# One ScalarE table load per run of tanh in a hybrid RWKV-7 and attention block

## The chip, the cores and the metric

The kernel runs on one core of a Trainium2 chip. A core has five engines that run on their own and meet at semaphores: TensorE (PE in the rows; its weight loads are PEld), VectorE (DVE), ScalarE (ACT), GpSimd (POOL) and SyncE (SP), which only issues DMA transfers here. ScalarE and POOL issue some DMAs too. The metric is the device time of one execution in microseconds (us), lower is better.

## The reference

One layer of a block over T = 528 tokens (512 of the input behind 16 learned ones) with 1024 features, all in float32:

```python
u = rmsnorm(h, norm_mix)
proj = u @ w_in                      # 5384 columns: RWKV, attention, two gates
y_rw = rwkv7_branch(...)             # 8 heads of 64: delta rule over time, group norm
y_fx = fox_branch(...)               # 8 heads of 64: softmax(q k' / 8 + F_q - F_k) v
merged = sigmoid(gA) * (y_rw @ w_out_rw) + sigmoid(gB) * (y_fx @ w_out_fx)
h = h + merged @ w_o
z = rmsnorm(h, norm_mlp)
h = h + square(relu(z @ w_up)) @ w_down
```

The functions that matter here are those that ScalarE evaluates from a table. The RWKV branch has `tanh` and `sigmoid` (decay, in-context rate and gate) and normalises its keys by a root. The attention branch normalises every head of q and k by a root and takes `exp` in the softmax. F is the running sum of `log_sigmoid`.

## The kernel before

**Tables.** The kernel writes a sigmoid as `0.5 tanh(x/2) + 0.5` and a reciprocal root as `exp(-0.5 ln(x))`. ScalarE holds one set of functions at a time. `natural_log_exp_and_others` has both logarithm and exponential; tanh stands in another set, which also has the exponential. Where the function of the next instruction isn't in the set that is held, the compiler puts an `ACT_TABLE_LOAD` ahead of it. The kernel also places loads itself: `pinned(prev)` (L253 to L257) issues a load of `natural_log_exp_and_others`, ordered behind the instruction `prev`, and its callers order their first logarithm behind that load. The callers are `normed` (L527, the root for q and k of one pair of attention heads, Ln at L528 and Exp at L530), `Pair.keys` (L710, Ln at L711 and Exp at L712) and the end of the mixing stage (L1080).

**Stages.** From 0 to 40 us the kernel normalises the input. From 40 to about 480 us one long stage computes 24 projections of features, 16 of gates, the RWKV branch and the attention. From there to about 577 us come the two output projections and the second norm, and after that the MLP, which is TensorE's work almost without a break.

**The long stage** is made of streams (Python generators) that a planner takes turns with: `projections` (matmuls at L476; their weights are split into a high and a low part, `whi` by ScalarE's cast at L447 and `wlo` by GpSimd at L448), `recurrent` for four pairs of RWKV heads, `chain` (the recurrence over nine chunks of 64 tokens, L871 to L920), `group_norm` (L928 to L954), `fox_features` (q and k) and `attention`. The planner fixes the order of TensorE's instructions by hand. On the other engines the framework's scheduler orders the instructions by priority and its own estimate of time, so a load more or less can change that order.

**Names.** In `Pair.keys`: `okk` the keys, `sq` their squares and then the root, `tm` the shifted copy that L306 makes of a projection in PSUM (`pj`), which VectorE's L307 combines (`orr` for r, `ov` for v); L715, L719 to L721 and L730 to L732 build the recurrence's factors. In `chain`, per chunk: matmul L887 into `pch`, VectorE copies `Rs` (L889), matmul L893, VectorE copies `uv` (L895), matmul L908, VectorE adds `SP` (L910), ScalarE prepares the next `uv` (L875) and `SP` (L903) and takes out `y_rw` (L920). In `group_norm`: sums L930, mean L931, subtraction L932, ScalarE's squares `ysq` (L934), sums L936, a root by iteration (L937, L220 to L227), scaling L939. In attention: L591 and L589 work on scores `psc`, L594 is the softmax's Exp, L614 and L626 are small copies from PSUM. L1022 are DMAs that ScalarE issues for sums of the last stage's weights, and L487 takes out a gate's projection (`gt`).

Of the kernel before, what the change touches and what calls it, by code (L numbers as in the profile page):

```python
# [13 lines left out]
AF = mybir.ActivationFunctionType  # L14
# [174 lines left out]
def kernel(ctx, tc, ht, x, win, par, cst, gain, lora, wout, wo, wup, wdn, out, dbg=None):  # L189
    nc = tc.nc  # L190
    dbg = dbg or {}
    mm = nc.tensor.matmul
    act = nc.scalar.activation
# [17 lines left out]
    prh = cp.tile([128, 4, 4], F32, name="prh")  # L211
# [28 lines left out]
    def load_w(src, low=(V, V)):  # L240

        return [load_h(src[:, 512 * j:512 * j + 512], low[j], "w", (4, 4, 4)) for j in range(2)]

    def wk(w, k):

        return [x[:, 128 * (k % 4):128 * (k % 4) + 128] for x in w[k // 4]]

    def after(ins, prev):

        tc.add_manual_dep(ins.ins, prev.ins.name, mybir.DependencyInfo(mybir.DependencyClass.NoSync, mybir.DependencyReason.DATA),  # L250
                          reason="one accumulation at a time")

    def pinned(prev):  # L253

        p = nc.scalar.preload_act_table_set("natural_log_exp_and_others")
        after(p, prev)
        return p  # L257

    def split(hi, lo, x):
        A.copy(hi, x)  # L260
# [2 lines left out]
    def passes(w, x):  # L263
        return ((w[0], x[0]), (w[0], x[1]), (w[1], x[0]))
# [6 lines left out]
    with ExitStack() as st:  # L271
# [6 lines left out]
        def psm(name="psm"):  # L278
            return ps.tile([128, 512], F32, name=name, tag="sm", bufs=4)
# [135 lines left out]
        def banks(n):  # L415
            return ck.ring("sm", n, 4)
# [80 lines left out]
        def fox_features():  # L497
            for p in range(4):
# [19 lines left out]
                def normed(d, parts, gcol):  # L518
                    yield d["in"]
                    f, sq = d["f"], d["sq"]  # L520
                    yield lambda: max(ck.ready(sq), banks(len(parts)))
                    pin = None
                    for a0, a1 in parts:
                        pq = psm("pssq")[:, :a1 - a0]
                        for hs in hss:
                            mm(pq[hs], ones_blk[hs, hs], sq[hs, a0:a1], start=True, stop=True)
                        pin = pin or pinned(d["s"])  # L527
                        after(act(sq[:, a0:a1], pq, AF.Ln, bias=eps, scale=1.0 / 64), pin)  # L528
                    c0 = parts[0][0]
                    act(sq[:, c0:], sq[:, c0:], AF.Exp, scale=-0.5)  # L530
                    V.scalar_tensor_tensor(f, f, gcol, sq[:, c0:], ALU.mult, ALU.mult)
                    return f
# [107 lines left out]
        def pad(t):  # L640
            G.memset(t[:, :PADT], 0.0)
            return t[:, PADT:]

        def load_lora(p, part, bufs):
            raw = rp.tile([128, 128], F32, name="lraw", tag="yT")
            nc.sync.dma_start(raw, lora[p][:, 128 * part:128 * part + 128])
            lw = [wp.tile([128, 128], F32R, name=f"lw{part}{i}", bufs=bufs) for i in range(2)]
            split(lw[0], lw[1], raw)
            return lw
# [3 lines left out]
        class Pair:  # L653
# [20 lines left out]
            def decay(self):  # L674
                p = self.p
                lw = load_lora(p, 0, 1)

                self.sg = sg = rp.tile([128, TP], F32, name="sg")
                self.tha = rp.tile([128, TP], F32, name="tha")
                dst = [pad(sg), pad(self.tha)]  # L680
                for a0, a1 in ((0, HT), (HT, T)):
                    yield lambda: max(ck.ready(*lw), banks(2))
                    pos = [psm("pup")[:, :HT] for i in range(2)]
                    for n, (wi, xi) in enumerate(((0, 0), (0, 1), (1, 0))):
                        for po, hs in zip(pos, hss):
                            mm(po, lw[wi][hs], (lhi, llo)[xi][hs, 0, a0:a1], start=n == 0, stop=n == 2)
                    for i in range(2):
                        act(dst[i][:, a0:a1], pos[i], AF.Tanh, bias=prh[:, i, p:p + 1], scale=0.5)
                V.tensor_scalar(dst[0], dst[0], 0.5, 0.5, ALU.mult, ALU.add)
                self.lc = lc = rp.tile([128, TP], F32, name="lc")  # L690
                V.tensor_tensor_scan(lc, smask.rearrange("p a b -> p (a b)"), sg, 0.0, ALU.mult, ALU.add)
                self.P = P = rp.tile([128, NCH, 64], F32, name="P")
                act(P.rearrange("p a b -> p (a b)"), lc, AF.Exp, scale=-CDEC)
                act(lc, lc, AF.Exp, scale=CDEC)
                self.pend = rp.tile([128, NCH], F32, name="pend", bufs=4)
                V.tensor_copy(self.pend, P[:, :, 63])

            def keys(self):

                p = self.p  # L700
                okr, thr, kp, pinv = self.okk[:, PADT:], self.tha[:, PADT:], self.sg, v9(self.lc)
                self.sq = sq = rp.tile([128, TP], F32, name="sq")
                s_ = act(sq[:, :T], okr, AF.Square, scale=self.col(C_KK))
                yield lambda: max(ck.ready(sq), banks(2))
                for hc in (slice(0, HT), slice(HT, T)):
                    pq = psm("pkk")[:, :HT]
                    for hs in hss:
                        mm(pq[hs], ones_blk[hs, hs], sq[hs, hc], start=True, stop=True)
                    V.tensor_scalar(sq[:, hc], pq, 1e-24, None, ALU.max)
                pin = pinned(s_)  # L710
                after(act(sq[:, :T], sq[:, :T], AF.Ln), pin)  # L711
                act(sq[:, :T], sq[:, :T], AF.Exp, scale=-0.5)  # L712
                V.tensor_scalar(kp[:, PADT:], thr, prh[:, 2, p:p + 1], prh[:, 3, p:p + 1], ALU.mult, ALU.add)
                V.tensor_tensor(kp[:, PADT:], kp[:, PADT:], okr, ALU.mult)
                V.scalar_tensor_tensor(okr, okr, self.col(C_KK), sq[:, :T], ALU.mult, ALU.mult)  # L715
                kkn, kp3, tha3 = v9(self.okk), v9(kp), v9(self.tha)

                self.BK = BK = rp.tile([128, NCH, 3, 64], F32, name="BK", tag="BK")
                V.scalar_tensor_tensor(BK[:, :, 2, :], kkn, 0.5, pinv, ALU.mult, ALU.mult)  # L719
                V.scalar_tensor_tensor(BK[:, :, 0, :], tha3, 1.0, BK[:, :, 2, :], ALU.add, ALU.mult)  # L720
                A.copy(BK[:, :, 2, :], BK[:, :, 0, :])  # L721
                G.tensor_tensor(BK[:, :, 1, :], kp3, pinv, ALU.mult)
# [317 lines left out]
    def ppo():  # L1040
        return ps.tile([128, 512], F32, name="po")
# [4 lines left out]
    with ExitStack() as st:  # L1046
# [3 lines left out]
                split(yhi[:, 4 * j + k, :], ylo[:, 4 * j + k, :], src[:, k, :])  # L1050
        mhi = mp.tile([128, KB, S], F32R, name="mhi")
        mlo = mp.tile([128, KB, S], F32R, name="mlo")
        for m in range(KB):
            w = load_w(wout[m])
            pp = []
            for br in range(2):
                g = mp.tile([128, S], F32, name=f"gl{br}", bufs=2)
                nc.sync.dma_start(g, gates_d[8 * br + m])
                act(g, g, AF.Tanh, scale=0.5)
                po = ppo()  # L1060
                n = 0
                for k in range(4 * br, 4 * br + 4):
                    for a, b in passes(wk(w, k), (yhi, ylo)):
                        mm(po, a, b[:, k, :], start=n == 0, stop=n == 11)  # L1064
                        n += 1
                V.scalar_tensor_tensor(g, g, 1.0, po, ALU.add, ALU.mult)
                pp.append(g)
            G.tensor_tensor(pp[0], pp[0], pp[1], ALU.add)
            merged = act(mhi[:, m, :], pp[0], AF.Copy, scale=0.5)
            V.scalar_tensor_tensor(mlo[:, m, :], pp[0], 0.5, mhi[:, m, :].bitcast(F32), ALU.mult, ALU.subtract)  # L1070
# [7 lines left out]
        zhi = hp.tile([128, KB, S], F32R, name="zhi", tag="zhi")  # L1078
        zlo = hp.tile([128, KB, S], F32R, name="zlo", tag="zlo")
        pin = pinned(merged)  # L1080
        early = []
        for j in range(2):
# [53 lines left out]
    with ExitStack() as st:  # L1136
# [50 lines left out]
        for p0, n_pairs in zip(FIRST, SLICES):  # L1187
# [4 lines left out]
            if p0 == 0:  # L1192

                ws, pos = early + [load_w(wup[2])], [ppo() for i in range(3)]
# [169 lines left out]
```

## Time and profile before

| | |
|---|---|
| median of 3 runs | 913.06 us |
| lowest and highest of them | 909.12 and 915.47 us |
| profiled execution, device time | 908.14 us |
| its span in the profile | 906.1 us |
| mean granted TensorE clock | 0.976 |
| TensorE busy | 862.7 us (95%) |
| VectorE busy | 594.3 us (66%) |
| ScalarE busy | 462.1 us (51%) |

The profile is one execution. A row of the timeline gives start, duration, engine, source line, operation, what is written from what, and in square brackets how long the engine had been idle and on whom it waited. The chain of waits follows the work that ended last back from the end; time on it is time of the kernel, time beside it is not. In the view by stretches the columns behind each stretch are its length, the busy time of PE, PEld, DVE, ACT and POOL with counts, the granted TensorE clock, the share of the DMA engines and GB/s.

### The profile page before, as it was taken

What the parts mean: (1) busy time and instruction counts of PE and PEld (TensorE: products, weight loads), DVE (VectorE), ACT (ScalarE), POOL (GpSimd) and SP (SyncE); (2) the same over time, 40 slices, a digit from 0 to 9 for tenths busy, and PEclk for the clock granted to TensorE, in tenths of its full rate; (3) what the DMA queues carried; (4) which work ended last, traced back from release to release, by engine and by line L of the source; (5) the groups of instructions that cost most, each with busy time, mean ns of one, the idle gap of its engine ahead of it and who ended that gap; (6) DMA issues with size and microseconds to landing.
All of it is one profiled execution on the core that took longest, in us unless ns stands there. A gap on an engine that the chain in (4) does not pass through costs nothing.

```text
span 906.1 us, 15737 instructions
## 1 busy us (share of the span) xinstructions
PE 862.7 (95%) x5896; PEld 702.6 (78%) x5896; DVE 594.3 (66%) x1168; ACT 462.1 (51%) x937; POOL 177.2 (20%) x169
## 2 busy tenths in 40 slices
PE   7889898999899999998989999999999999999998
PEld 6878786767797777676857877988888888888886
DVE  7965894447968794455476756377556675566776
ACT  7837243786355532675364644255444554344542
POOL 1154552223544353322301210000000000000000
PEclk9999998999999999999988999999999999999999
DMA  6223547475753467674685643034632366522564
GB/s 211 69 73 96 139 103 207 108 168 136 164 141 97 113 188 182 164 188 106 164 249 186 206 160 95 1 93 147 194 113 93 96 194 192 151 99 94 152 214 169
DMA packets 69771, 129.46 MB, mean 143 GB/s; under 512 B 6840, under 2 KB 7992, under 8 KB 69696
## 3 DMA queue, kind: packets, MB, share of 16 engines
q1 hardware_dynamic: 52288, 94.91, 32.9%
q0 software_dynamic: 8704, 16.78, 11.6%
q10 hardware_dynamic: 8704, 16.78, 5.6%
q8 instruction: 46, 0.75, 0.3%
q14 instruction: 29, 0.24, 0.1%
HBM read 122.13 MB, written 39.86 MB: 179 GB/s over the span
## 4 chain that ended last, share of the span: by engine, by line
PE 72%; DVE 15%; ACT 3%; issue 3%; DMA 2%; POOLq 0%; POOL 0%; ACTq 0%; SPq 0%; DVEq 0%
PE po L1143 19%; PE pj L476 16%; PE po L1233 12%; PE pd L1233 5%; PE po L1064 3%; PE po L1113 2%; PE pw L828 2%; DVE tmp L810 1%; PE psc L580 1%; PE py L625 1%; DVE AX L822 1%; PE pbt L776 1%; DVE Tt L822 1%; DVE AX L811 1%; DVE L L730 1%
## 5 line engine op out<-in xcount | busy, mean ns | idle before, releaser
L237 DVE TENSOR_TENSOR wlo<-wraw,whi 128x512 fp32r<-128x512 f32 x200 | 140.3, 708 | 95.8 <-ACT whi L236 95.5
L236 ACT CAST whi<-wraw 128x512 fp32r<-128x512 f32 x200 | 123.7, 621 | 135.8 <-PE po L1143 43.0
L476 PE MATMUL pj<-uhi,whi 128*128 128x264 f32 (+1 forms) x480 | 170.0, 354 | 11.0 <-DVE orr L307 3.9
L476 PE MATMUL pj<-ulo,whi 128*128 128x264 f32 (+1 forms) x480 | 157.5, 328 | 0.6 <-DVE ulo L390 0.6
L476 PE MATMUL pj<-uhi,wlo 128*128 128x264 f32 (+1 forms) x480 | 156.9, 327 | 0.0
L448 POOL TENSOR_TENSOR wlo<-wraw,whi 128x512 fp32r<-128x512 f32 x76 | 104.4, 1383 | 162.2 <-ACT whi L447 143.6
L476 PEld LDWEIGHTS pj<-uhi,whi 128*128 128x128 f32 x480 | 93.1, 194 | 32.7 <-issue 11.3
L476 PEld LDWEIGHTS pj<-uhi,wlo 128*128 128x128 f32 x480 | 93.4, 195 | 7.3
L476 PEld LDWEIGHTS pj<-ulo,whi 128*128 128x128 f32 x480 | 93.6, 195 | 5.4 <-DVE ulo L390 1.1
L1143 PE MATMUL po<-zhi,whi 128*128 128x512 f32 (+1 forms) x248 | 94.8, 382 | 0.0
L1143 PE MATMUL po<-zlo,whi 128*128 128x512 f32 (+1 forms) x248 | 94.8, 382 | 0.0
L1143 PE MATMUL po<-zhi,wlo 128*128 128x512 f32 (+1 forms) x248 | 94.8, 382 | 0.0
L447 ACT CAST whi<-wraw 128x512 fp32r<-128x512 f32 x80 | 49.2, 618 | 45.0 <-PE pj L476 27.3
L1233 PE MATMUL po<-wlo,fhi 128*128 128x512 f32 x160 | 62.4, 390 | 0.0
L1233 PE MATMUL po<-whi,flo 128*128 128x512 f32 x160 | 62.3, 389 | 0.0
L1233 PE MATMUL po<-whi,fhi 128*128 128x512 f32 x160 | 62.2, 389 | 0.0
L1143 PEld LDWEIGHTS po<-zhi,wlo 128*128 128x128 f32 x248 | 46.6, 188 | 9.1
L1143 PEld LDWEIGHTS po<-zlo,whi 128*128 128x128 f32 x248 | 46.6, 188 | 9.0
L1143 PEld LDWEIGHTS po<-zhi,whi 128*128 128x128 f32 x248 | 46.6, 188 | 8.9
L1155 ACT CAST fhi<-R 128x768 fp32r<-128x768 f32 (+1 forms) x32 | 30.2, 943 | 24.0 <-DVE R L1162 13.6
L1156 DVE TENSOR_TENSOR flo<-R,fhi 128x768 fp32r<-128x768 f32 (+1 forms) x32 | 34.8, 1089 | 7.8 <-ACT fhi L1155 7.8
L1233 PEld LDWEIGHTS po<-wlo,fhi 128*128 128x128 f32 x160 | 30.0, 188 | 6.5 <-DVE wlo L237 0.3
(292 smaller groups left out, 1658.9 us busy)
## 6 DMA issues: line engine op xcount, KB each, us to landing
wraw<-in_win SPq DMA_DIRECT2D x84, 256.0 KB, 3.0
tsum<-in_wdn ACTq DMA_DIRECT2D x32, 512.0 KB, 4.3
wraw<-in_wup SPq DMA_DIRECT2D x64, 256.0 KB, 2.6
wraw<-tsum SPq DMA_DIRECT2D x64, 256.0 KB, 2.8
wraw<-in_wdn SPq DMA_DIRECT2D x48, 256.0 KB, 2.7
tsum<-in_wdn POOLq DMA_DIRECT2D x16, 512.0 KB, 7.6
tsum<-tsum POOLq DMA_DIRECT2D x16, 512.0 KB, 6.3
gd<-gt SPq DMA_DIRECT2D x16, 256.0 KB, 2.3
```

The lines of the kernel that those rows point to most:

```text
L236: A.copy(hi, raw)
L237: low.tensor_tensor(lo, raw, hi.bitcast(F32), ALU.subtract)
L447: A.copy(hi, raw)
L448: low.tensor_tensor(lo, raw, hi.bitcast(F32), ALU.subtract)
L476: mm(po, a, b[:, k, a0:a1], start=n == 0, stop=n == 23)
L822: V.tensor_copy(dst[rs_, :, o:o + 32], src[rs_, :, :n2].rearrange("p t n -> p n t"))
L828: mm(ps_[hs, n - b0, :], lhs(n)[hs], rhs(n)[hs], start=True, stop=True)
L1064: mm(po, a, b[:, k, :], start=n == 0, stop=n == 11)
L1143: mm(po[:, t0:t1], a, b[:, k, t0:t1], start=n == 0, stop=n == 23)
L1155: A.copy(fhi[:, j, a:b], R[:, a:b])
L1156: V.tensor_tensor(flo[:, j, a:b], R[:, a:b], fhi[:, j, a:b].bitcast(F32), ALU.subtract)
L1233: mm(x[i], a[:, k, left, 128 * i:128 * i + 128], c, start=start and k == 0 and n == 0, stop=stop and k == n_pairs - 1 and n == 2)
```

## The change

A list keeps the tanh instructions that were issued since the kernel's last load. `pinned` issues a load only if that list isn't empty or if there has been none yet; otherwise it hands back the load that was issued last, and the callers order their logarithm behind that one. A new load is ordered behind all the tanh in the list. The tanh of the recurrent stream (L688) goes through the new helper. Ahead of the output projections, whose tanh (L1059) doesn't go through it, the remembered load is forgotten, so that L1080 issues one.

```diff
+    table = {"tanh": [], "pin": None}
+
+    def tanh(*args, **kw):
+        x = act(*args, func=AF.Tanh, **kw)
+        table["tanh"].append(x)
+        return x
+
     def pinned(prev):
 
-        p = nc.scalar.preload_act_table_set("natural_log_exp_and_others")
-        after(p, prev)
-        return p
+        if table["tanh"] or table["pin"] is None:
+            p = nc.scalar.preload_act_table_set("natural_log_exp_and_others")
+            after(p, prev)
+            for x in table["tanh"]:
+                after(p, x)
+            table["tanh"], table["pin"] = [], p
+        return table["pin"]
...
-                        act(dst[i][:, a0:a1], pos[i], AF.Tanh, bias=prh[:, i, p:p + 1], scale=0.5)
+                        tanh(dst[i][:, a0:a1], pos[i], bias=prh[:, i, p:p + 1], scale=0.5)
...
         mlo = mp.tile([128, KB, S], F32R, name="mlo")
+        table["pin"] = None
         for m in range(KB):
```

In the built kernels ScalarE's list has 21 table loads before and 11 in the change. TensorE's, GpSimd's and SyncE's lists read alike but for line numbers; VectorE's differs in the place of a few instructions. Lines of the changed kernel stand 11 further on (12 from L1064), its own loads are L263, and the tanh of L688 and the loads ahead of them are L256. Three places, each of before and then of the change:

Place A, ScalarE, the keys of the second pair (some 85 to 97 us in the trace of before):

```order
L703 ACTIVATE sq<-okk,pr 128x528
L255 ACT_TABLE_LOAD
L1022 DMA tsum_105<-in_wdn 256x512
L711 ACTIVATE sq<-sq 128x528
L306 ACTIVATE tm<-pj,pr 128x264
L712 ACTIVATE sq<-sq 128x528
```

```order
L714 ACTIVATE sq<-okk,pr 128x528
L1033 DMA tsum_105<-in_wdn 256x512
L317 ACTIVATE tm<-pj,pr 128x264
L722 ACTIVATE sq<-sq 128x528
L723 ACTIVATE sq<-sq 128x528
```

The load is gone, and the copy `tm`, which stood between the logarithm and the exponential, stands ahead of both.

Place B, ScalarE, roots of q and k in the second attention pair, with the recurrence beside it (some 179 to 193 us):

```order
L903 ACTIVATE SP<-uv,pend 64x64 x4
L530 ACT_TABLE_LOAD
L530 ACTIVATE fsq<-fsq 128x512
L512 ACTIVATE fsq<-pj 128x264
L513 COPY ka<-pj 128x264
L447 CAST whi<-wraw 128x512
L594 ACTIVATE pe,rsum<-pe,nm 128x528
L1022 DMA tsum_107<-in_wdn 256x512
L875 COPY uv<-pvt 64x2x128 x2
L594 ACTIVATE pe,rsum<-pe,nm 128x528
L626 COPY y_fx<-py 128x128
L255 ACT_TABLE_LOAD
```

```order
L914 ACTIVATE SP<-uv,pend 64x64 x4
L541 ACTIVATE fsq<-fsq 128x512
L523 ACTIVATE fsq<-pj 128x264
L524 COPY ka<-pj 128x264
L458 CAST whi<-wraw 128x512
L1033 DMA tsum_107<-in_wdn 256x512
L886 COPY uv<-pvt 64x2x128 x2
L605 ACTIVATE pe,rsum<-pe,nm 128x528 x2
L637 COPY y_fx<-py 128x128
L458 CAST whi<-wraw 128x512
```

Ahead of the first row the compiler's load for L528 is replaced by one of the kernel's; the compiler's load for L530 and the kernel's at the end are gone. Where the latter stood, ahead of the next `SP`, there is now the cast of a weight that came seven rows later before.

VectorE at the same place:

```order
L589 TENSOR_TENSOR psc<-psc,cs 128x128
L591 ISA pe,nm<-psc,nF_1516,nm 128x256
L591 ISA nm 128x1
L531 SCALAR_TENSOR_TENSOR qa<-qa,qg_67,fsq 128x512
L889 COPY Rs<-pch 128x128
```

```order
L600 TENSOR_TENSOR psc<-psc,cs 128x128
L542 SCALAR_TENSOR_TENSOR qa<-qa,qg_67,fsq 128x512
L602 ISA pe,nm<-psc,nF_1514,nm 128x256
L602 ISA nm 128x1
L900 COPY Rs<-pch 128x128
```

The scaling of q, which needs the root, stands ahead of a reduction of scores that stood ahead of it; `Rs` comes behind both as before.

Place C, ScalarE, the root of q in the last attention pair, with a group norm beside it (some 403 to 411 us):

```order
L255 ACT_TABLE_LOAD
L528 ACTIVATE fsq<-pssq,eps 128x512
L903 ACTIVATE SP<-uv,pend 64x64 x4
L920 COPY y_rw<-pyy 128x2x64
L530 ACTIVATE fsq<-fsq 128x512
L512 ACTIVATE fsq<-pj 128x264
L513 COPY ka<-pj 128x264
L875 COPY uv<-pvt 64x2x128 x2
L626 COPY y_fx<-py 128x128
L934 ACTIVATE ysq<-y_rw 128x512
L1022 DMA tsum_119<-in_wdn 256x512
```

```order
L539 ACTIVATE fsq<-pssq,eps 128x512
L541 ACTIVATE fsq<-fsq 128x512
L914 ACTIVATE SP<-uv,pend 64x64 x4
L931 COPY y_rw<-pyy 128x2x64
L523 ACTIVATE fsq<-pj 128x264
L524 COPY ka<-pj 128x264
L886 COPY uv<-pvt 64x2x128 x2
L945 ACTIVATE ysq<-y_rw 128x512
L637 COPY y_fx<-py 128x128
L1033 DMA tsum_119<-in_wdn 256x512
```

The load is gone, the two halves of the root follow each other, and the group norm's squares `ysq` stand ahead of the copy `y_fx` instead of behind it.

VectorE at the same place:

```order
L930 TENSOR_REDUCE st_4917<-y_rw 128x8
L889 COPY Rs<-pch 128x128
L531 SCALAR_TENSOR_TENSOR qa<-qa,qg_67,fsq 128x512
L895 COPY uv<-pch 64x128 x2
L931 TENSOR_SCALAR st_4917<-st_4917 128x8
L932 TENSOR_TENSOR y_rw<-y_rw,st_4917 128x2x256
L936 TENSOR_REDUCE st_4923<-ysq 128x8
L910 TENSOR_TENSOR uv<-pch,SP 64x128 x2
```

```order
L542 SCALAR_TENSOR_TENSOR qa<-qa,qg_67,fsq 128x512
L941 TENSOR_REDUCE st_4910<-y_rw 128x8
L900 COPY Rs<-pch 128x128
L942 TENSOR_SCALAR st_4910<-st_4910 128x8
L943 TENSOR_TENSOR y_rw<-y_rw,st_4910 128x2x256
L906 COPY uv<-pch 64x128 x2
L947 TENSOR_REDUCE st_4916<-ysq 128x8
L948 TENSOR_SCALAR st_4916<-st_4916 128x8
```

The scaling of q and the copies of `uv` no longer stand between the group norm's sums and its subtraction, and `uv`'s sum (L910, L921 in the change) falls three short instructions back.

## The prediction

> **What bounds the kernel now.** I read the page's head and its chain of waits first, then ScalarE's groups by line, then the timeline around each load.
>
> ```profile
> span 906.1 us, 15737 instructions
> ...
> PE 72%; DVE 15%; ACT 3%; issue 3%; DMA 2%; POOLq 0%; POOL 0%; ACTq 0%; SPq 0%; DVEq 0%
> ```
>
> TensorE holds 72% of the chain that sets the end, VectorE 15%, ScalarE 3%. So a load costs time only where TensorE or VectorE stands and waits for what is queued behind it. The profiled execution took 908.14 us, 2.0 more than its span; the median of the runs is 913.06, 4.9 above it. I work out a difference from the profiled execution and take it off the median.
>
> ScalarE's table loads, by the line of the instruction that needs them (L255 are the kernel's own):
>
> ```profile
> L255 ACT ACT_TABLE_LOAD x13 | 16.7, 1283 | 0.2
> ...
> L688 ACT ACT_TABLE_LOAD x3 | 3.8, 1283 | 11.8 <-PE pup L686 11.8
> ...
> L379 ACT ACT_TABLE_LOAD x1 | 1.3, 1283 | 0.0
> L528 ACT ACT_TABLE_LOAD x1 | 1.3, 1283 | 0.0
> L530 ACT ACT_TABLE_LOAD x1 | 1.3, 1283 | 0.0
> L1059 ACT ACT_TABLE_LOAD x1 | 1.3, 1283 | 1.7 <-DMA gl<-gd 1.7
> ```
>
> With the first load of the program these are 21, each 1.283 us. The change leaves 11: ten go, 10 x 1.283 = 12.8 us of ScalarE's time, and that is the most that the loads by themselves can give. All ten lie in the long stage. In the chain of waits only one of them shows:
>
> ```profile
> 179.65 1.28 ACT L528
> ...
> 182.71 1.28 ACT L530
> ```
>
> The first of these two is replaced by a load of the kernel's at the same place and costs what it cost. The second goes. The other nine stand beside the chain. Seven of them I cost at nothing: behind them ScalarE waits for another engine anyway, as here behind the load for the third pair's q,
>
> ```profile
> 302.40 0.69 ACT L528 ACTIVATE fsq<-pssq,eps 128x512 f32<-128x512 f32 x1 [3.34 <-PE pssq L526]
> ```
>
> where it then stood idle for 3.34 us, more than twice a load, or what it hands on isn't what TensorE's fixed order waits for next. If that cover were gone each would cost up to 1.28 us. The two that are left matter only because the scheduler filled ScalarE's order anew around them; these are places A and C.
>
> **Place A: one copy out of the way, 0.37 us.** ScalarE, then VectorE:
>
> ```profile
> 88.68 0.65 ACT L711 ACTIVATE sq<-sq 128x528 f32<-128x528 f32 x1 [0.95 <-DVE sq L709]
> 89.23 0.47 ACT L306 ACTIVATE tm<-pj,pr 128x264 f32<-128x264 f32 x1
> 89.59 0.64 ACT L712 ACTIVATE sq<-sq 128x528 f32<-128x528 f32 x1
> ```
>
> ```profile
> 90.26 0.77 DVE L715 SCALAR_TENSOR_TENSOR okk<-okk,pr,sq 128x528 f32<-128x528 f32 x1
> ```
>
> The load ahead of L711 is covered: ScalarE then waited 0.95 us for VectorE. But L306 stood between L711 and L712 and took 89.59 - 89.23 = 0.36 of the queue. In the change it runs in that 0.95 (its matmuls stand ahead of those that L709 needs on TensorE, so its input is there). L712 ends at 90.23 and VectorE starts L715 at 90.26, so L715 and the recurrence's factors behind it come 0.37 earlier. TensorE waits for them. Bounds: 0, if a cast's `wlo` on GpSimd, which also comes earlier, holds VectorE; 0.9, if it gets out of VectorE's way. I take 0.37.
>
> **Place B: a load of 1.28 gives 0.69 us.** VectorE's order, then TensorE:
>
> ```profile
> 183.14 0.48 DVE L591 CUSTOM_DVE_ANT_0 pe<-psc,nF,nm 128x256 f32<-128x256 f32 x1
> ...
> 184.67 0.75 DVE L531 SCALAR_TENSOR_TENSOR qa<-qa,qg,fsq 128x512 f32<-128x512 f32 x1 [1.04 <-ACT fsq L530]
> 185.34 0.28 DVE L889 COPY Rs<-pch 128x128 f32<-128x128 f32 x1
> ```
>
> ```profile
> 185.68 0.45 PE L893 MATMUL pch<-Rs,Tt 64*64 64x64 f32 x8 [1.04 <-DVE Rs L889]
> ```
>
> Without the load L530 ends 1.28 earlier, and L531 can start at 184.67 - 1.28 = 183.39. In the change L591 stands behind it and no longer fills the wait: 183.39 + 0.75 + 0.48 + some 0.03 between them gives 184.65 for `Rs`, against 185.34. So TensorE's L893 comes 0.69 earlier. More than the 1.04 that TensorE waited can't come of it, and nothing comes of it if the softmax's Exp, which falls behind `uv` on ScalarE, is then late. Ends: 0 and 1.04; I take 0.69, which the rows give.
>
> The Trainium skill ("ScalarE: Activation LUTs", What ACT_TABLE_LOAD costs) gives a switch of sets 1283 ns and about 1380 ns of drain, 2.66 us in all. The row at 182.71 agrees with the first figure and shows no drain: L530 runs right behind the load in the chain. By the page the ten loads would be worth 26.6 us of ScalarE and this place its whole 1.04, an estimate.
>
> **Place C: a wait of VectorE and GpSimd, 2.28 us, and a slow clock, 1.40 us.** ScalarE first, then VectorE, GpSimd and TensorE:
>
> ```profile
> 408.61 0.74 ACT L875 COPY uv<-pvt 64x256 f32<-64x256 f32 x2
> ...
> 410.17 0.64 ACT L934 ACTIVATE ysq<-y_rw 128x512 f32<-128x512 f32 x1
> ```
>
> ```profile
> 410.84 0.69 DVE L936 TENSOR_REDUCE st<-ysq 128x8 f32<-128x512 f32 x1 [1.02 <-ACT ysq L934]
> ...
> 414.41 1.30 DVE L227 TENSOR_SCALAR rsgy<-rsgy 128x8 f32<-128x8 f32 x1
> 415.74 1.71 DVE L939 TENSOR_TENSOR y_rw<-y_rw,rsgy 128x512 f32<-128x512 f32 x1
> 417.48 0.29 DVE L889 COPY Rs<-pch 128x128 f32<-128x128 f32 x1
> ```
>
> ```profile
> 414.39 2.51 POOL L448 TENSOR_TENSOR wlo<-wraw,whi 128x512 fp32r<-128x512 f32 x2 [10.86 <-ACT whi L447]
> ```
>
> ```profile
> 417.82 0.45 PE L893 MATMUL pch<-Rs,Tt 64*64 64x64 f32 x8 [2.28 <-DVE Rs L889]
> ```
>
> With the load gone the root of q is done sooner, and the squares stand right behind L875: they start at 408.61 + 0.74 = 409.35 instead of 410.17, 0.82 earlier. (Their input, the subtraction on VectorE, now has L531 and the copies of `uv` out of its way.) The group norm's root then runs 0.82 earlier, and L227 comes at 413.59. Before, it began 0.02 behind GpSimd's two `wlo` and took 1.30 us for 8 elements a row, and L939 took 1.71 for 512, where L936 takes 0.69 for as many: both stood until GpSimd was through. At 413.59 L227 is ahead of GpSimd. That start, 414.39, hangs on ScalarE's cast, which follows the copies of `SP`, which follow L910; and L910 falls three short instructions back, at (3.57 - 0.69) / 12 = 0.24 each (410.84 to 414.41, twelve instructions behind L936), so GpSimd gains only 0.1 or so. `Rs` is then ready before TensorE needs it, and the wait of 2.28 goes whole. If GpSimd still catches them, 0.82 is left. I take 2.28.
>
> After that wait TensorE ran slow; after a shorter one in the same loop it did not. The rows are the stretch behind this wait, then the other wait with the stretch behind it:
>
> ```profile
> 418.00:422.00 4.00, 4.00 (x43) 2.58 (x42) 1.15 (x4) 2.22 (x7) 0.00 (x0) 0.65 0.96 193
> ```
>
> ```profile
> 218.47 0.45 PE L893 MATMUL pch<-Rs,Tt 64*64 64x64 f32 x8 [1.43 <-DVE Rs L889]
> ```
>
> ```profile
> 220.00:224.00 4.00, 4.00 (x52) 2.93 (x51) 2.18 (x6) 3.34 (x10) 0.53 (x1) 1.00 0.00 0
> ```
>
> The granted clock was 0.65 behind the wait of 2.28 us and 1.00 behind that of 1.43. Four microseconds at 0.65 lose 4 x 0.35 = 1.40 us. Even if only 0.82 goes, the wait is 1.46, next to the one without a loss, so I count the 1.40; the ends are 0 and 1.40.
>
> The Trainium skill ("TensorE: Matmul & The Clock Gate", Part 1: The HAM clock gate) has the clock halved after an idle window of about 3.4 us, free-running. The row shows it reduced behind 2.28 us already. By that rule taken literally a shorter wait changes nothing in the clock, and the sum would lack 1.40 us; that case is weighed among the rivals.
>
> **The sum.** 0.37 + 0.69 + 2.28 + 1.40 = 4.74 us. Behind each place the chain runs on through TensorE, whose order is unchanged, so a shift there is kept; the last 330 us are TensorE's alone. 908.14 - 4.74 = 903.4 for a run like the profiled one, 913.06 - 4.74 = 908.3 for the median.
>
> **The rivals.**
>
> - *Only the bare shifts.* GpSimd still stands in VectorE's way at C, so that 0.82 of the wait goes, and the clock falls all the same because what counts is the phase of its window. Then 0.37 + 0.69 + 0.82 = 1.88, 911.2 us. For it: GpSimd and VectorE are some 0.7 apart at the crossing, and a small delay turns it. Against: 1.46 stands next to the 1.43 that cost nothing. Chance 0.27 with all between it and the forecast's lower part.
> - *ScalarE is closer to the bound than the chain shows.* Five of the nine covered loads have work of other streams right behind them with little or no idle time. If each of these brings its 1.28, that is 5 x 1.283 = 6.4 on top, 11.2 in all, 901.9 us. All ten on the path and the terms at C would give some 896. For it: in the stretch around B ScalarE was back to back. Against: TensorE has its own work there, and the chain passes none of them. Chance 0.15.
> - *A cast blocks ScalarE, and the kernel is slower.* At B the weight's cast moves into the place of a load:
>
> ```profile
> 188.66 1.28 ACT L255 ACT_TABLE_LOAD   x1
> ...
> 194.10 0.61 ACT L447 CAST whi<-wraw 128x512 fp32r<-128x512 f32 x1
> ```
>
>   ScalarE works in order. If the buffer that this cast writes were still being read by TensorE, or its weight not yet loaded, everything behind it (`SP` and `uv` of the recurrence, the root of k) would wait, at worst until 194.10: 194.10 - 188.66 = 5.44 us, and TensorE with it. It decides against the kernel above the 4.74 that the rest gives: 913.8 us, and 916.6 if C gives only 0.82 without the clock. Against it: that the cast stood at 194.10 was the scheduler's place for it, not a wait (its row has no idle time), and with four buffers the one it writes held a weight that TensorE was half through by then. Chance 0.06.
> - *The change doesn't do what it says.* The compiler could put loads back where a logarithm meets the wrong set, as it did at L528 and L530. The order of the change shows 11 loads and none of the compiler's in front of a logarithm, so I give this no chance of its own.
>
> **How the numbers follow.** The forecast has 0.45, the bare shifts 0.27, more loads on the path 0.15, the blocked cast 0.06; 0.07 stays for the clock falling in other places once the phases have moved. The likeliest is 908.3 us. Its own range goes from the bounds of its terms, 4.74 with A at 0.9 and B at 1.04, 5.6 (907.5), to 1.88 (911.2). The runs before lay between 909.12 and 915.47, some 0.4% to either side, and that is added in part. The low end takes in most of the second rival, 901.5; the high end takes in the third's smaller price, 914.5. One per cent, 9.1 us, is about what a measurement of this kernel can tell from no change. Faster by more than that needs the second rival or the forecast with a run to run spread in its favour: 0.19. Slower by more than that, over 922.2 us, needs the blocked cast with something on top: 0.03. Within: 0.78.
>
> **What would show it.** ScalarE with 11 loads and some 449 us busy (462.1 less 12.8). At A, L306 ahead of L711, and L715 some 0.03 behind the end of L712. At B, TensorE's L893 with a wait of some 0.35 us instead of 1.04. At C, L227 in some 0.2 us, L939 near 0.7, the wait at L893 gone or under 0.5, and a clock of 1.00 in the four microseconds behind it. A span of some 901.4. The forecast is wrong if GpSimd's `wlo` still lies over L227 at C, if the clock is below 0.9 in stretches where it was 1.00, or if ScalarE stands at the moved cast with a wait for TensorE or a DMA.

## The result, and the profile after

The changed kernel takes 904.01 us (median of 11 runs, 902.41 to 907.24), the kernel before 910.57 us (11 runs): a ratio of 0.993, 95% interval 0.9907 to 0.9953. On another chip it was 906.41 against 911.6, 0.9946 (0.9918 to 0.9973). So it is half a per cent to 0.7% faster, within the one per cent for which the forecast had its largest chance. The profiled span went from 906.1 to 901.0 us, 5.1 less; the forecast was a span of 901.4 and a median of 908.3.

The page of the changed kernel, its head and its chain of waits, and then ScalarE's table loads by line (busy, mean ns | idle before):

```profile
span 901.0 us, 15730 instructions
...
PE 858.4 (95%) x5896; PEld 699.2 (78%) x5896; DVE 593.8 (66%) x1168; ACT 449.3 (50%) x927; POOL 175.9 (20%) x169
...
PE 69%; DVE 15%; DMA 4%; ACT 4%; issue 3%; POOLq 0%; POOL 0%; ACTq 0%; SPq 0%; DVEq 0%
...
L263 ACT ACT_TABLE_LOAD x5 | 6.4, 1283 | 0.1
L256 ACT ACT_TABLE_LOAD x3 | 3.8, 1283 | 12.5 <-PE pup L697 12.5
```

With three more of one each these are 11 loads, and ScalarE is 449.3 us busy: both as forecast. ScalarE lost 12.8 us of work and the kernel 5.1.

Place B and then place C in the changed kernel, by the timeline; B is TensorE alone, C is VectorE, GpSimd and TensorE:

```profile
184.73 0.40 PE L487 MATMUL pj<-uhi,wlo 128*128 128x512 f32 x1
185.26 0.45 PE L904 MATMUL pch<-Rs,Tt 64*64 64x64 f32 x8
```

```profile
412.68 0.17 DVE L227 TENSOR_SCALAR rsgy<-rsgy 128x8 f32<-128x8 f32 x1
412.89 0.69 DVE L950 TENSOR_TENSOR y_rw<-y_rw,rsgy 128x512 f32<-128x512 f32 x1
413.77 0.29 DVE L900 COPY Rs<-pch 128x128 f32<-128x128 f32 x1 [0.19 <-PE pch L898]
```

```profile
413.29 2.67 POOL L459 TENSOR_TENSOR wlo<-wraw,whi 128x512 fp32r<-128x512 f32 x2 [10.68 <-PE pj L487]
```

```profile
414.55 0.45 PE L904 MATMUL pch<-Rs,Tt 64*64 64x64 f32 x8
```

Neither row of L904 shows a wait for `Rs` any more (1.04 and 2.28 us before). L227 takes 0.17 us and the multiplication L950 0.69, where they took 1.30 and 1.71: both now start ahead of GpSimd (412.68 and 412.89 against 413.29), and it takes its turn behind them. The clock behind it is whole, in the number behind the busy times (1.00, the granted clock):

```profile
412.00:416.00 4.00, 4.00 (x41) 2.85 (x39) 2.28 (x9) 2.95 (x9) 2.71 (x3) 1.00 0.10 40
416.00:420.00 4.00, 4.00 (x52) 2.60 (x49) 1.67 (x5) 2.94 (x9) 0.76 (x1) 1.00 0.80 162
```

Place A went the other way. VectorE, GpSimd and TensorE of the changed kernel:

```profile
96.28 3.75 DVE L743 TENSOR_TENSOR L<-orr,P 64x576 f32<-64x576 f32 x2
```

```profile
98.14 1.27 POOL L459 TENSOR_TENSOR wlo<-wraw,whi 128x512 fp32r<-128x512 f32 x1 [0.37 <-ACT whi L458]
```

```profile
100.17 1.57 PE L772 MATMUL psr<-L,BK 64*128 64x128 f32 x22 [0.83 <-DVE tm L314]
```

and VectorE and GpSimd before:

```profile
96.57 2.63 DVE L732 TENSOR_TENSOR L<-orr,P 64x576 f32<-64x576 f32 x2
```

```profile
98.44 3.19 POOL L448 TENSOR_TENSOR wlo<-wraw,whi 128x512 fp32r<-128x512 f32 x2 [0.38 <-ACT whi L447]
```

VectorE's two products for `L` took 2.63 us and take 3.75. GpSimd's `wlo` got in ahead of the second one, which then stood until GpSimd was through; TensorE waits 0.83 us for what follows. Here a gain of 0.37 was forecast.

**How the places were measured.** TensorE's list is the same in all kernels here, so its nth matmul in one trace is the nth in the other. The difference of their starts moves in steps, each with a place. The table gives these steps in us against the profiled execution of the kernel before, worked out from the matmul records (A: 91 to 103 us, B: 180 to 194, C: 409 to 425), the number of clock windows at half speed (below), and the span. The rows are the kernels of the next section; a second and third row of a kernel is another profiled execution.

| kernel | A | B | C | slow windows | span |
|---|---|---|---|---|---|
| before | 0 | 0 | 0 | 12 | 906.1 |
| before, 2nd | +1.12 | -0.01 | +0.02 | 11 | 909.9 |
| changed | +0.77 | -0.77 | -3.81 | 9 | 901.0 |
| changed, 2nd | +0.76 | -0.79 | -3.80 | 12 | 907.3 |
| changed, 3rd | -0.36 | -0.78 | -3.80 | 12 | 904.1 |
| r_a | +0.01 | -0.79 | -3.80 | 7 | 898.6 |
| r_c | +0.77 | -0.79 | +1.28 | 14 | 908.0 |
| r_all | +1.11 | -0.81 | -1.47 | 8 | 906.1 |
| e_edges | +1.46 | +0.01 | -2.93 | 12 | 905.0 |
| r_rest | +0.76 | -0.79 | -3.81 | 12 | 905.4 |
| e_fixa | -0.34 | -0.78 | -3.81 | 9 | 902.2 |
| e_fixa, 2nd | -0.34 | -0.78 | -3.80 | 12 | 905.2 |
| e_mlp | +0.76 | -0.76 | -3.80 | 12 | 908.3 |

Between the places the difference is flat to some hundredths of a microsecond, but for other slow windows and smaller crossings like that of A. Spans of one kernel lie up to 6.3 us apart, so a single span tells little here, and the steps tell much. The ratios below are the recorded ones, with their 95% intervals; they aren't the quotients of the two medians given beside them, from which they differ by up to 0.4% (e_fixa: 0.9878 recorded, 0.9917 by medians).

### The profile page after: what moved, and what is told of

Read it like the earlier page. It is cut to its first block, busy times and chain, and to the rows that moved or that the text cites. A ratio compares the mean times of both kernels' runs of the same rounds, so it can differ in the third digit from the quotient of the medians.

```text
span 901.0 us, 15730 instructions
## 1 busy us (share of the span) xinstructions
PE 858.4 (95%) x5896; PEld 699.2 (78%) x5896; DVE 593.8 (66%) x1168; ACT 449.3 (50%) x927; POOL 175.9 (20%) x169
## 4 chain that ended last, share of the span: by engine, by line
PE 69%; DVE 15%; DMA 4%; ACT 4%; issue 3%; POOLq 0%; POOL 0%; ACTq 0%; SPq 0%; DVEq 0%
PE po L1155 19%; PE pj L487 16%; PE po L1245 11%; PE pd L1245 5%; PE po L1125 2%; PE po L1076 2%; PE pw L839 2%; DMA wraw<-in_wo 1%; DVE tmp L821 1%; PE py L636 1%; DVE AX L833 1%; PE pbt L787 1%; PE psc L591 1%; DVE Tt L833 1%; DVE L L743 1%
```

## The experiments

### Loads put back one place at a time

Four kernels are the changed one with a list of places at which a load is issued all the same:

```diff
-    def pinned(prev):
+    def pinned(prev, place=None):
-        if table["tanh"] or table["pin"] is None:
+        if place in KEEP or table["tanh"] or table["pin"] is None:
...
+KEEP = ("keys1",)                    # r_a
+KEEP = ("q3", "k3")                  # r_c
+KEEP = ("keys1", "k0", "q1", "k1", "keys2", "q2", "k2", "q3", "k3")   # r_all
+KEEP = ("k0", "keys2", "q2", "k2")   # r_rest
```

**r_a, the load at place A.**

> The changed kernel with one of the ten loads put back, the one ahead of the logarithm of the second pair's keys (place A). ScalarE's order there is then that of before: the copy tm between logarithm and exponential, so L715 of before comes 0.3 later again, the cast whi too, and GpSimd's wlo should start behind VectorE's second copy of the convolution's output instead of ahead of it. Theory (the crossing at A costs the change some 0.9): the load put back makes the kernel faster than the changed one, a span of about 900.1 us against 901.0, VectorE's two copies in 2.63 instead of 3.75, and TensorE's matmul that waits for gt at about 142.7 instead of 143.6. Rival (a load costs its time on ScalarE): span 901.0 + 1.28 = 902.3. No effect beyond the noise of a profile would be 901.0 within 0.3.

Ratio to before 0.9929 (0.9895 to 0.9964), median 907.17 against 912.4. At A the two products took 2.64 us and TensorE's step was +0.01, so it looks as the theory said. But the span of 898.6, below the 900.1 expected, goes with only 7 slow windows, and the next kernels showed that the load is not what decided at A.

**r_c, the two loads of the last attention pair.**

> The changed kernel with the loads ahead of q's and k's logarithm in the last attention pair put back (place C, two loads). The squares ysq then stand behind the copy y_fx again. Theory (order at C sets the crossing with GpSimd): TensorE's wait for Rs of about 2.3 us near 413 to 418 returns, and a granted clock of 0.6 to 0.8 in the 4 us behind it; L227 takes over 1 us again; the span is 901.0 + 3.8 = 904.8 us. Rival (the gain at C is the loads' own time): 2 x 1.28 = 2.6, span 903.6, with no return of the slow clock. If neither order nor load matters there, 901.0.

Ratio 0.9989 (0.9957 to 1.0022), median 910.73: with these two loads back the gain is gone to within the interval. VectorE and TensorE of r_c at C:

```profile
412.87 1.29 DVE L228 TENSOR_SCALAR rsgy<-rsgy 128x8 f32<-128x8 f32 x1
414.19 1.71 DVE L951 TENSOR_TENSOR y_rw<-y_rw,rsgy 128x512 f32<-128x512 f32 x1
```

```profile
416.28 0.69 PE L905 MATMUL pch<-Rs,Tt 64*64 64x64 f32 x8 [2.27 <-DVE Rs L901]
```

The wait is back, 2.27 us, with the old durations of both instructions, and two slow windows behind it. TensorE's step at C is 1.28 + 3.81 = 5.1 us worse than in the changed kernel; without the second slow window it would be the 3.8 of the theory. The loads' own time, 2.6, is out.

**r_all, all nine places of the kernel's own loads.** One of the nine, the second pair's q, has its load in the changed kernel too, so the trace has 19 loads, eight more than the changed kernel and two fewer than before.

> The changed kernel with all nine of its own covered loads put back; against before only place B differs, where one load of the kernel's and two of the compiler's are now one, and VectorE scales q (L531 of before) ahead of the reduction of scores (L591). It isolates B. Theory: B gives the 1.28 us of a load, because the wait of 1.04 at TensorE goes and the stages behind it are kept; at A the order of before (no loss), at C the order of before (wait 2.28 and slow clock there): span 906.1 - 1.28 = 904.8 us. The prediction's own term for B would give 906.1 - 0.69 = 905.4. Rival (each load costs its time on the path): 901.0 + 9 x 1.28 = 912.5.

Ratio 0.9973 (0.9936 to 1.001), median 909.52, span 906.1. At B the wait is gone and the step is -0.81, close to the prediction's term and not the 1.28 of a load. The rival's 912.5 (911.2 with eight loads) is out. What the order on VectorE would give at B without taking a load away was not tried. Two things were not expected. At A the products took 3.75 us although ScalarE's order there was that of before. And at C the wait was as long as before, but the clock was whole behind it (see the clock, below).

**r_rest, four of the loads costed at nothing.**

> The changed kernel with four of the loads put back that the prediction costed at nothing: before the roots of k of the first pair, of q and k of the third, and before the logarithm of the third pair's keys. Theory (behind them ScalarE waits for another engine anyway): 0 us by the loads themselves, TensorE's steps as in the changed kernel within 0.3 us up to place C, apart from slow clock; span 901.0 give or take the 1.7 us that one slow window of the clock costs. Rival (a load costs its time on ScalarE): 4 x 1.28 = 5.1 us more, 906.1.

Ratio 0.9928 (0.9902 to 0.9954), median 905.64 against 911.12 on its chip. ScalarE's loads are

```profile
L264 ACT ACT_TABLE_LOAD x9 | 11.5, 1283 | 0.1
```

9 where the changed kernel has 5, and the ratio is that of the changed kernel. Its steps at A, B and C are the changed kernel's within 0.02. The span, 905.4, lies near the rival's 906.1 and outside what the theory allowed, but it has 12 slow windows, and the changed kernel's own two profiles with 12 of them took 904.1 and 907.3. So the span decides nothing here. The steps and the ratio do: the four loads cost nothing that can be seen.

### Order alone, with all 21 loads

e_edges is the kernel before with two edges of order at C:

```diff
-                    A.copy(y_fx[:, p, 128 * i:128 * i + 128], py)
+                    taken = A.copy(y_fx[:, p, 128 * i:128 * i + 128], py)
+                    if (p, i) == (2, 3):
+                        after(taken, marked["ysq"])
...
-                    V.tensor_copy(uv[hs, 0, e], ch[hs, 1])
+                    u_ = V.tensor_copy(uv[hs, 0, e], ch[hs, 1])
+                    if (g, c, e) == (1, 5, 0):
+                        after(u_, marked["centred"])
```

> The kernel before with all its 21 loads; two edges of order are added at place C only: the copy y_fx stands behind the squares ysq, and the copy uv on VectorE behind the subtraction that makes ysq's input. Theory (C's gain is a matter of order, not of a load): GpSimd's wlo no longer catches L227, the wait of 2.28 at TensorE goes, the clock stays 1.00 behind it, and the span is 906.1 - 3.7 = 902.4 us. Rival (the load's 1.28 in front of q's root is what delays ysq, and stays): ysq comes at most 0.4 earlier, GpSimd still stands in the way, span 905.7 to 906.1.

VectorE, GpSimd and TensorE of e_edges at C:

```profile
414.99 0.17 DVE L227 TENSOR_SCALAR rsgy<-rsgy 128x8 f32<-128x8 f32 x1
415.20 1.81 DVE L949 TENSOR_TENSOR y_rw<-y_rw,rsgy 128x512 f32<-128x512 f32 x1
```

```profile
415.18 2.96 POOL L450 TENSOR_TENSOR wlo<-wraw,whi 128x512 fp32r<-128x512 f32 x2 [10.62 <-PE pj L478]
```

```profile
417.39 0.45 PE L897 MATMUL pch<-Rs,Tt 64*64 64x64 f32 x8 [0.81 <-DVE Rs L893]
```

The 8-element L227 got ahead of GpSimd, the multiplication behind it did not, by 0.02 us. The wait fell from 2.28 to 0.81 and the clock stayed whole: 2.93 of the 3.81 us came without a load removed.

ScalarE's squares and VectorE's sum for `uv`, in e_edges and then that sum in the changed kernel:

```profile
410.32 0.63 ACT L942 ACTIVATE ysq<-y_rw 128x512 f32<-128x512 f32 x1
```

```profile
412.35 0.59 DVE L916 TENSOR_TENSOR uv<-pch,SP 64x128 f32<-64x128 f32 x2 [0.47 <-PE pch L914]
```

```profile
410.45 0.59 DVE L921 TENSOR_TENSOR uv<-pch,SP 64x128 f32<-64x128 f32 x2
```

At C e_edges ran 1.03 us behind before. Put back by that, its squares began at 410.32 - 1.03 = 409.29, 0.88 earlier than before and no later than in the changed kernel (409.38, worked out below). So the load in front of q's root doesn't hold them up, and the rival, 0.4 at most, is out. What e_edges lacks of the changed kernel's gain lies behind the squares, on VectorE: there the sum for `uv` still stands ahead of the root's steps and waits 0.47 us for TensorE, and L227 comes 0.36 later than in the changed kernel, which has that sum two short instructions further back and no wait. No run moves this sum alone, so that last part is read from the rows and not shown.

The median is 908.54 against 912.4, a quotient of 0.9958, but the recorded ratio, 0.9988 (0.996 to 1.0016), doesn't separate e_edges from before. The span, 905.0 against the 902.4 expected, has as many slow windows as before, 12, but one of them lies at A. So by the steps the mechanism at C is order, as the theory had it.

### The crossing at A

> The kernel before, unchanged, for a second look at the clock. Theory (the clock is granted for windows of 3.41 us whose phase differs from one execution to the next; a window in which TensorE is busy for less than about half is followed by one at half clock): the same waits as in the first look within 0.1 us where no slow window falls, among them 2.2 to 2.3 us at place C; the slow windows lie elsewhere than in the first look, and behind the wait at C the clock is 1.00 if the wait is split between two windows and 0.5 for 3.41 us if it lies in one. Rival (a wait of over 2 us brings the slow clock by itself): the stretch behind the wait at C is slow again as in the first look, 0.65 over 4 us.

> The changed kernel, unchanged, for a second look. Theory (the crossing at A is decided by hundredths of a microsecond): GpSimd's wlo may be on either side of VectorE's second copy; if it is ahead the two copies take 3.75 us and TensorE stands 0.83 us, if behind 2.63 and no such wait. B and C as in the first look: no wait of over 0.5 us for Rs near 185 and near 414. Rival (the crossing at A follows from the order of the changed kernel): 3.75 again, and the gains at B or C missing in this look would put them down to chance as well.

The kernel before, unchanged, took 909.9 us in its second profile, and there it lost the crossing too: its two products took 3.75 us,

```profile
96.80 3.75 DVE L732 TENSOR_TENSOR L<-orr,P 64x576 f32<-64x576 f32 x2
```

```profile
98.66 1.27 POOL L448 TENSOR_TENSOR wlo<-wraw,whi 128x512 fp32r<-128x512 f32 x1 [0.35 <-ACT whi L447]
```

and its step is +1.12. The changed kernel lost it in the second profile (span 907.3), and won it in the third. VectorE's second product is due 1.88 us behind the start of the first. By the records, in the seven executions that lost, `wlo` began 10 to 30 ns ahead of the second product; in the three that won without an edge (before, r_a, the third of the changed kernel) within some 3 ns of that due time. So the crossing falls one way or the other within one kernel, before the change as behind it; two and three executions can't tell whether the change shifts the odds. In e_edges a slow window lay over A, the cast ahead of `wlo` waited 1.36 us for TensorE instead of 0.38, and `wlo` came too late to cross.

e_fixa makes it certain: GpSimd's `wlo` waits for the second product. No engine's order changes.

```diff
-                low.tensor_tensor(lo, raw, hi.bitcast(F32), ALU.subtract)
+                sub = low.tensor_tensor(lo, raw, hi.bitcast(F32), ALU.subtract)
+                if len(converted) == 9 and not w:
+                    after(sub, marked["L"], "Sync")
...
-                    V.tensor_tensor(l1[hs, :, 64:128], r3[hs], P[hs], ALU.mult)
+                    copied = V.tensor_tensor(l1[hs, :, 64:128], r3[hs], P[hs], ALU.mult)
+                    if (self.p, e) == (1, 1):
+                        marked["L"] = copied
```

> The changed kernel, no load put back, with one more edge: GpSimd's first wlo behind place A waits for VectorE's second copy of the convolution's output (L743). No engine's order changes. Theory (what A loses is GpSimd's wlo getting between VectorE's two copies, whatever the number of loads): the two copies take 2.63 us together as before the change, not 3.75; TensorE's 0.83 wait for tm behind them goes, and TensorE is 0.9 us earlier there than in the changed kernel; the wlo itself is 0.8 later, which nobody waits for. By the clock's share in the rest, a span of 900.1 against 901.0. Rival (the loss at A has another cause, as the kernel with nine loads put back, which also showed 3.75, may suggest): the wait stays, or the later wlo is waited for and the gain is nothing.

VectorE, GpSimd and TensorE of e_fixa:

```profile
96.85 2.64 DVE L749 TENSOR_TENSOR L<-orr,P 64x576 f32<-64x576 f32 x2
```

```profile
99.72 2.52 POOL L460 TENSOR_TENSOR wlo<-wraw,whi 128x512 fp32r<-128x512 f32 x2 [1.36 <-DVE tm L315]
```

```profile
99.44 1.77 PE L783 MATMUL psr<-L,BK 64*128 64x128 f32 x24
```

The products take 2.64 us, the wait of 0.83 is gone and nobody waits for the later `wlo`. TensorE's step is -0.34 in both of its profiles and -0.36 in the profile of the changed kernel that won by itself. With +0.77 where it lost, a lost crossing costs 0.77 + 0.35 = 1.12 us, which is just what it cost the kernel before in its second profile. The rest, 0.35, is what the moved copy `tm` gives, on either side of the crossing.

Timed, e_fixa was at 0.9878 (0.9827 to 0.993) in 4 runs. It was then timed again beside the changed kernel on one chip:

> The changed kernel, timed beside the one with the edge at A and the one with extra loads. Theory: against the kernel before 4.3 to 6.5 us faster (B 0.8, C 2.3, slow clock behind C 1.2 on average, and what the order around 210 us brings), 0.993 to 0.995; in its profile 3.75 us for VectorE's two copies at A more likely than 2.63.

> The changed kernel with the edge at A, timed on the same chip as the changed kernel alone. Theory: 1.1 us faster than that one where it would lose the crossing, 0 where not, so 0.5 to 1.1 us in the mean, ratio to before 0.992 to 0.994. Rival (the 6.5 us between the two means seen so far, on different chips, is the edge's own): a ratio of 0.988 again on this chip, with the changed kernel at 0.993.

The changed kernel: 0.9946 (0.9918 to 0.9973), 906.41 us. With the edge: 0.9951 (0.9926 to 0.9976), 906.16 us, outside the 0.992 to 0.994 expected. So the 0.9878 was chance, or its chip's, and the edge's 1.12 us in executions that would have lost the crossing is too little for these intervals. No kernel here is shown to beat the changed one.

### Ten more loads where TensorE never waits

```diff
-            act(r, po, AF.Relu)
+            relu = act(r, po, AF.Relu)
+            if len(extra) < 10:
+                extra.append(nc.scalar.preload_act_table_set("natural_log_exp_and_others"))
+                after(extra[-1], relu)
```

> The changed kernel with ten more table loads, all in the stage of the up projections, where TensorE is busy without a break. Theory (a load costs nothing where ScalarE's order has room): ScalarE is busy 12.8 us longer, TensorE's steps in that stage stay within 0.1 us of those of the changed kernel, and the time stays within 1 us. Rival (a load costs its time): 12.8 us slower.

ScalarE's loads at the added line:

```profile
L1164 ACT ACT_TABLE_LOAD x10 | 12.8, 1283 | 0.2
```

The time is 907.0 us against 906.41 for the changed kernel on the same chip, ratio to before 0.9968 (0.9939 to 0.9997): within the 1 us expected and not 12.8. In the matmul records TensorE's difference to the kernel before moves from 1.02 us at 565 us to 1.15 at 676, over all ten loads (587.5 to 669.8), and no further to 880: 0.13, just over the 0.1 expected. As many loads as the change removed, put elsewhere, cost next to nothing.

### The clock

The granted clock changes only at multiples of 3.41 us, in every trace here, and where these lie against the program differs from one execution to the next. Cut at these bounds, the windows around the wait at C show it. Columns: window, its length, busy time (and count) of TensorE's matmuls, its weight loads, VectorE, ScalarE and GpSimd, granted clock, DMA share, GB/s. First before, then r_all, which has a wait of the same length there (2.27 us, from 413.60 to 415.87):

```profile
412.34:415.75 3.41, 3.21 (x27) 2.50 (x26) 3.00 (x13) 3.32 (x10) 1.36 (x2) 1.00 0.26 99
415.75:419.16 3.41, 1.34 (x16) 0.91 (x18) 2.57 (x4) 1.53 (x3) 1.96 (x2) 1.00 0.37 88
419.16:422.58 3.42, 3.42 (x32) 2.29 (x29) 0.58 (x2) 2.27 (x7) 0.00 (x0) 0.50 0.80 142
```

```profile
411.45:414.86 3.41, 2.15 (x19) 1.45 (x17) 3.21 (x7) 3.34 (x6) 2.42 (x2) 1.00 0.05 17
414.86:418.27 3.41, 2.40 (x36) 1.51 (x36) 1.58 (x5) 1.57 (x4) 0.89 (x2) 1.00 0.70 139
418.27:421.69 3.42, 3.42 (x36) 2.35 (x35) 1.47 (x4) 2.17 (x8) 0.87 (x1) 1.00 0.90 225
```

Before, the wait lay in one window, TensorE was busy 1.34 of 3.41 us in it, 39%, and the next window ran at half clock. In r_all the bound fell into the wait, both windows were busy over 60%, and no slow window followed. The second profile of before again had the wait in one window (1.18 of 3.41 busy) and one slow window behind it, so its rival, that a wait of over 2 us does it by itself, is out by r_all alone.

Over the 13 profiles, from about 10 us on, where the traces' record of the clock begins, of the windows at full clock that were busy less than 45% (matmuls), all 51 were followed by one at half clock; of those between 45% and 65%, 26 of 70; of those above, 2 of some 3,100. A slow window costs up to 3.41 / 2 = 1.7 us, less where TensorE would have waited in it anyway. A program here has 7 to 14 of them. Over the 31 runs of the kernel before that were timed beside e_edges, the mean granted clock (0.967 to 0.986) goes with 79% of the variance of the time, so most of the spread from run to run goes with the clock.

## Why the prediction was right, and where not

The median, 904.01, lies in the range (901.5 to 914.5) and the ratio within one per cent. By its own steps:

- **What bounds, and the seven loads at nothing: right.** Loads count only where TensorE or VectorE waits for what stands behind them. r_rest shows it for four of the seven, e_mlp for ten loads elsewhere. Of the other three, two are back in r_all and bring no step of their own; the third, at 158.90 in the trace of before, is gone in the changed kernel, and the difference stays at 0.46 to 0.47 us from 150 to 180.
- **Place A, 0.37: the size was right, the bound wrong.** The moved `tm` gives 0.34 to 0.36. The step that failed is the lower bound, "0, if a cast's `wlo` on GpSimd, which also comes earlier, holds VectorE". A lost crossing doesn't cancel the gain, it costs 1.12 us. And whether it is lost isn't a matter of this change: the kernel before stood within nanoseconds of it and won it in the profile that I read.
- **Place B, 0.69: too small, 0.88 at L904, of which 0.78 stays.** L531 of before started where forecast. The term behind it was mis-sized: I added durations, 0.75 + 0.48 + 0.03 = 1.26, but instructions of VectorE start before the one ahead has ended:

```profile
183.85 0.75 DVE L542 SCALAR_TENSOR_TENSOR qa<-qa,qg,fsq 128x512 f32<-128x512 f32 x1 [0.29 <-ACT fsq L541]
184.52 0.48 DVE L602 CUSTOM_DVE_ANT_0 pe<-psc,nF,nm 128x256 f32<-128x256 f32 x1
...
184.92 0.28 DVE L900 COPY Rs<-pch 128x128 f32<-128x128 f32 x1
```

  From start to start it is 0.67 + 0.40 = 1.07, and the 0.19 between is the error. The prediction's own rows have the first of these steps, 184.67 to 185.34.
- **Place C, the wait of 2.28: right, to hundredths.** At C the changed kernel ran 0.92 us ahead of before. Put back by that, L945 began at 408.46 + 0.92 = 409.38 (forecast 409.35), L227 at 413.60 (413.59), and GpSimd at 414.21 (some 414.3). r_c takes it back, and e_edges gives most of it by order alone. The prediction put the earlier squares down to the missing load; in e_edges they come as early with the load in place, so what moved them is the order on ScalarE and VectorE.
- **Place C, the clock, 1.40: 1.53 in this pair of profiles, for the wrong reason.** I compared waits, 2.28 with a slow stretch and 1.43 without. By the counts above the next window's clock goes with TensorE's share of a window that has a phase of its own. The same wait was followed by one slow window, by two and by none. The rival of the bare shifts had this doubt in it ("what counts is the phase of its window"). The Trainium skill ("TensorE: Matmul & The Clock Gate", Part 1: The HAM clock gate) has a free-running window of about 3.4 us; the traces agree with that, 3.41. They differ from its idle window in that windows up to 45% busy never kept the clock, 51 of 51.
- **The sum.** The lasting parts are 0.35 + 0.78 + 2.28, 3.4 us, and up to 1.53 of clock: 4.9, against the 4.74 forecast. That the first pair of spans differs by 5.1 is partly chance: A lost 0.77, the stage between 460 and 500 us gained 0.9 with slow windows fewer, and smaller crossings made the rest. One of these the prediction has no term for: at 210 us TensorE's step is -0.48 to -0.50 in all three profiles of the changed kernel. In the first of them VectorE's 8-element L931 (L942 there), which runs while GpSimd works on a `wlo`, takes 0.67 us instead of 1.22. It isn't shown to be the change's: e_edges, with all 21 loads, has the -0.50 too, and e_mlp, with the changed order there, has +0.21. The medians differ by 6.6 and, on the other chip, 5.2.
- **The rivals.** A load's time as such is out (r_rest, e_mlp), and so is the cast that blocks ScalarE: at 188.33 the moved cast runs with no wait ahead of it,

```profile
188.33 0.62 ACT L458 CAST whi<-wraw 128x512 fp32r<-128x512 f32 x1
```

  The compiler put no load back. The bare shifts are out for the wait at C, and half true for the clock.

## What to carry to other kernels

Count what is taken off a side engine at nothing until the row of the engine that waits for it is found; here 12.8 us of loads were worth some 3.4 us, 4.9 with the clock, most of it by the order of a few instructions at C. Where two engines delay each other, look at how close their starts lie before you call a term safe: a bound at such a crossing reaches below nothing, and one profile shows one side of it. When run to run spread is as large as the effect, compare the starts of the same instruction in two traces place by place; the changed kernel's steps at B and C repeated to 0.03 us where its spans lay 6 us apart.

## What the runs showed of the hardware that was not expected

- VectorE's product and GpSimd's subtraction delay each other by whole instructions, and 10 to 30 ns decide which goes first: VectorE's pair took 2.63 us or 3.75, GpSimd's first `wlo` 1.27 us when ahead and 1.90 when behind. The Trainium skill ("SBUF — State Buffer", SBUF: two separate sides) has a lock on a pair of ports that these two engines share, taken for a whole instruction by whichever starts first; the rows agree in that one waits out the other.
- The clock windows above: how busy TensorE is in one window of 3.41 us goes with the clock of the next, and a share under 45% was not enough in 51 of 51 cases.
